# First feed-forward of a two-layer trunk: gating products and sums of gated tiles on VectorE instead of GpSimd

## The chip, the cores and the metric

The kernel runs as one program on one core of a Trainium2 chip. The metric is the device time of one execution in microseconds. It is called in one launch and does everything in it: all weights are loaded from HBM, and the result is written back.

Engines are called by the names of the profile: PE (TensorE, with its weight load PEld), DVE (VectorE), ACT (ScalarE), POOL (GpSimd) and SP (SyncE, which issues the DMAs).

## The reference

Two layers over x of 1024 tokens by 1024 channels, float32. Layer 0 has a short gated convolution, layer 1 a forgetting attention, and each ends with a SwiGLU feed-forward of hidden width 2816. All sub-layers are wrapped in a modulation by a condition vector c and a layer norm:

```python
for l in range(DEPTH):
    sh1, sc1, g1, sh2, sc2, g2 = jnp.split(c_act @ w_ada[l] + b_ada[l], N_MOD, axis=-1)
    h = modulate(x, sh1, sc1)
    ...
    x = layer_norm(DEEPNORM_ALPHA * x + g1[:, None, :] * y, ln1_g[l], ln1_b[l])
    h = modulate(x, sh2, sc2)
    y = swiglu(h, ffn_w_gate[l], ffn_w_up[l], ffn_w_down[l])
    x = layer_norm(DEEPNORM_ALPHA * x + g2[:, None, :] * y, ln2_g[l], ln2_b[l])

def swiglu(h, w_gate, w_up, w_down):
    return (jax.nn.silu(h @ w_gate) * (h @ w_up)) @ w_down
```

The change is in the first line of this swiglu, for l = 0.

## The kernel before, in words

A float32 operand is split into a high part and a rest, and a product is three matmuls (`mm3`, lines 167 to 171): high by high, high by rest, rest by high. `split_f` (line 654) makes the parts of a weight block: ACT writes the high part (line 659), DVE the rest (line 660).

The first feed-forward (`first_ffn`, line 1300) multiplies in blocks, with seven block products in place of eight. Tokens are in two halves of 512, hidden channels in 22 tiles of 128, taken as 11 pairs j. `hidden` (line 833) computes the gate and the up product of a pair in slots named M1 to M7. A slot has two products (m = 0 gate, m = 1 up), 12 matmuls of 128x512 each, into PSUM banks X, Y or Z of the pair. For the first six pairs ("early") M1 and M2 run ahead in slots of their own; then each pair has the slots M5, M6, M3, M7 and, after the M5 of the next pair, its M4. The later pairs have M1 and M2 in line as well.

After each product comes its evacuation (`evac`, line 1026). M5 and M6 only keep a partial sum (`keep_sum`, line 962, on DVE). M2, M3, M7 and M4 each finish a tile of hidden values (`out`, line 972). For m = 0, DVE adds the bank and the kept sum (line 979) and ACT applies silu (line 980). For m = 1, DVE adds again (line 999) and the result is multiplied with the silu (line 1000, on POOL). Where nothing has to be added, line 997 multiplies straight from the bank, on DVE. A finished tile is stored to HBM, and `derive` (line 1005) forms sums and differences of finished tiles (line 1008, on POOL), which are stored too, since the down projection multiplies in blocks again and wants them as operands.

Each `store` (line 866) is put off to the end of the next slot and then issued by SP (line 868). SP has one queue, in order. The same queue issues the weight loads of the hidden products (line 681), the loads of the modulation weights (`ada_lq`, line 783), the reloads of stored tiles (lines 875 and 882) and the loads of the down projection (lines 1145 and 1155).

Beside this, from slot 28 on, DVE computes the modulation vectors needed later: a quarter of a weight block per slot (`ada_quarter`, lines 260 and 262), from the loads of line 783. POOL forms the sums of weight blocks that M5, M3 and M7 need (`sums`, line 914: lines 918, 919, 921 and 923, each 128x1024), and at the start of the down projection those of line 1190.

The order in which instructions stand on each engine is fixed when the kernel is built. The build may move an instruction past others of its engine; at run time each engine takes its own in order. Tiles (`pg`) live in 47 pages of SBUF; a load into a page waits until its last reader is done.

Of the kernel before, what the change touches and what calls it, by code (L numbers as in the profile page):

```python
# [11 lines left out]
ALU = mybir.AluOpType  # L12
# [65 lines left out]
class Builder:  # L78
# [754 lines left out]
    def hidden(self, l, nearly, left):  # L833
# [3 lines left out]
        nc, T, look = self.nc, self.T, 2  # L837
        gp = nc.gpsimd
# [27 lines left out]
        def store(n, j, t):  # L866
            def fn():
                nc.sync.dma_start(self.dr[n][j * P:(j + 1) * P], t)
                self.stored.add((n, j))
            self.later(self.slot, fn)  # L870
# [93 lines left out]
        def leave(s, *names):  # L964
            for n in names:
                t = s.pop(n)
                if n in ("ya", "yb"):
                    self.later(self.slot, lambda t=t: self.drop("f", t))
                else:
                    self.drop("f", t)  # L970

        def out(j, r, half, s, m, bank, other):

            if m == 0:
                a = s["a"] = self.t("tmp", [P, HALF], tag="tA", bufs=3)
                if other is None:
                    nc.scalar.activation(a, bank, AF.Silu)
                else:
                    nc.vector.tensor_tensor(a, bank, other, op=ALU.add)  # L979
                    nc.scalar.activation(a, a, AF.Silu)  # L980
                return
            a = s.pop("a")
            if (r, half) == (0, 0):
                s["ya"] = self.fpage()
                y = s["ya"][:, 0]
            elif (r, half) == (1, 1):
                s["yb"] = self.fpage()
                y = s["yb"][:, 0]
            elif left and (r, half) == (0, 1):
                y = s["ya"][:, 1]  # L990
            elif (r, half) == (1, 0):
                self.flush(self.slot)
                y = s["yb"][:, 0]
            else:
                y = self.t("tmp", [P, HALF], tag="tB", bufs=3)
            if other is None:
                nc.vector.tensor_tensor(y, bank, a, op=ALU.mult)
            else:
                nc.vector.tensor_tensor(y, bank, other, op=ALU.add)
                gp.tensor_tensor(y, y, a, op=ALU.mult)  # L1000
            if (r, half) in asis:
                store(asis[r, half], j, y)
            derive(j, r, half, s, y)

        def derive(j, r, half, s, y):

            def tt(n, o, a, b, op=ALU.subtract):
                gp.tensor_tensor(o, a, b, op=op)
                if n:
                    store(n, j, o)  # L1010
            ya, yb = s.get("ya"), s.get("yb")
            if (r, half) == (0, 1) and not left:
                tt("M5", ya[:, 1], y, ya[:, 0])
            elif (r, half) == (1, 1):
                if left:
                    tt("M5", ya[:, 1], ya[:, 1], y, ALU.add)
                    tt("M6", yb[:, 1], ya[:, 1], ya[:, 0])
                    tt("M7", ya[:, 0], y, yb[:, 1])
                else:
                    tt("M6", yb[:, 1], y, ya[:, 1])  # L1020
                    tt("M7", ya[:, 0], yb[:, 1], ya[:, 0])
            elif (r, half) == (1, 0):
                tt("M3" if left else "M4", ya[:, 1], y, yb[:, 1])
                leave(s, "ya", "yb")

        def evac(i, m):
# [4 lines left out]
            if n == "M1":  # L1031
                keep(s, "m1", m, X)
                if e and m:
# [5 lines left out]
                    self.later(i, spill)  # L1039
            elif n == "M2" and e:  # L1040
                out(j, 0, 0, s, m, X, None)
                self.unbank(s.pop(("X", m)))
                if m:
                    leave(s, "ya")
            elif n == "M2":
                out(j, 0, 0, s, m, Z, s["m1"][:, m])
                self.unbank(s.pop(("Z", m)))
                if m:
                    leave(s, "m1")
            elif n == "M5":  # L1050
                keep_sum(s, "y5", m, Y, m1()) if e else keep(s, "y5", m, Y)
            elif n == "M6":
                keep_sum(s, "s2", m, X, m1()) if e else keep(s, "s2", m, X)
            elif n == "M3":
                if e and m:
                    s["ya"] = self.blk.pop(("b11", j)) if ("b11", j) in self.blk else None
                    if s["ya"] is None:
                        s["ya"] = self.lq_get(("b11", j))
                        self.blk.pop(("b11", j))
                out(j, 0, 1, s, m, Y, s["s2"][:, m])  # L1060
                self.unbank(s.pop(("Y", m)))
                if m:
                    leave(s, "s2")
            elif n == "M7":
                out(j, 1, 1, s, m, X, s["y5"][:, m])
                if m:
                    leave(s, "y5")
            elif n == "M4":
                out(j, 1, 0, s, m, X, m1() if e else None)
                self.unbank(s.pop(("X", m)))  # L1070
                if e and m:
                    self.lq_drop(("m1", j))
# [1056 lines left out]
```

## Time and profile before

| | us |
|---|---|
| median of 3 runs | 2519.61 (2512.10 to 2519.83) |
| the profiled execution | 2518.77 |
| its span, first to last instruction | 2517.0 |
| PE busy in the span | 2400.4 (95%) |
| DVE busy | 1497.8 (60%) |
| ACT busy | 827.3 (33%) |
| POOL busy | 860.0 (34%) |

The span is what the trace covers; the profiled execution's own time is 1.8 us longer. The first feed-forward's hidden part that the change touches runs from 510 to 911 us of the span. Shares over the whole span say little about it, since DVE is busy far more there than late in the kernel. Readings are therefore taken by stretches of the span.

### The profile page before, as it was taken

The numbers are of one execution on the slowest core, as the hardware profiler recorded it, in microseconds if no ns is written. First come the engines' busy times: TensorE is split into PE (matmuls) and PEld (weight loads), VectorE is DVE, ScalarE is ACT, GpSimd is POOL, SyncE is SP. The second block draws the span as 40 slices with busy tenths as digits, with TensorE's granted clock in tenths as the row PEclk, the third lists the DMA queues.
The fourth block names the chain that finished last, engine by engine and source line by source line (L and its number), as shares of the span: only waits on it lengthen the run. The fifth ranks groups of instructions, "written<-read, shape, count | busy, mean of one in ns | idle before, by whom it ended". The sixth has DMA issues, their size and how long they took to land. (4 is left out here: it accounts for less than half of the span.)

```text
span 2517.0 us, 29595 instructions
## 1 busy us (share of the span) xinstructions
PE 2400.4 (95%) x10905; PEld 1948.8 (77%) x10905; DVE 1497.8 (60%) x2129; ACT 827.3 (33%) x1321; POOL 860.0 (34%) x686
## 2 busy tenths in 40 slices
PE   7899999898899999999999999999999999999997
PEld 5688887687778878777777777777788888888886
DVE  5654548856788878986464667897632223232326
ACT  3311105421232333434223666665521111212113
POOL 6300002675556452343000556557330202030304
PEclk9999999999999999999999999999999999999999
DMA  8333303655575774215557555652211111111101
GB/s 269 118 101 117 92 17 97 202 163 173 174 225 173 272 249 147 83 51 194 192 179 226 174 176 145 153 133 72 67 34 51 51 51 51 51 43 50 44 32 67
DMA packets 286645, 311.95 MB, mean 124 GB/s; under 512 B 16068, under 2 KB 198548, under 8 KB 286500
## 3 DMA queue, kind: packets, MB, share of 16 engines
q1 hardware_dynamic: 274884, 284.69, 37.1%
q10 hardware_dynamic: 11616, 25.37, 2.7%
q8 instruction: 86, 1.41, 0.2%
q14 instruction: 59, 0.48, 0.1%
HBM read 252.91 MB, written 57.08 MB: 123 GB/s over the span
## 5 line engine op out<-in xcount | busy, mean ns | idle before, releaser
L169 PE MATMUL mm<-pg,pg 128*128 128x512 f32 x3004 | 1188.8, 397 | 35.8 <-DVE tA L979 11.4
L170 PE MATMUL mm<-pg,pg 128*128 128x512 f32 x3004 | 1186.1, 395 | 14.5 <-DVE pg L370 7.2
L171 PE MATMUL mm<-pg,pg 128*128 128x512 f32 x3004 | 1183.8, 394 | 3.6 <-POOL pg L368 2.6
L169 PEld LDWEIGHTS mm<-pg,pg 128*128 128x128 f32 x3004 | 571.7, 190 | 161.7 <-issue 18.2
L170 PEld LDWEIGHTS mm<-pg,pg 128*128 128x128 f32 x3004 | 571.8, 190 | 136.2 <-DVE pg L370 10.0
L171 PEld LDWEIGHTS mm<-pg,pg 128*128 128x128 f32 x3004 | 571.3, 190 | 125.2 <-POOL pg L368 4.1
L159 ACT CAST pg<-pg 128x1024 fp32r<-128x1024 f32 x144 | 150.5, 1052 | 586.2 <-PE mm L170 301.1
L660 DVE TENSOR_TENSOR pg<-pg,pg 128x1024 fp32r<-128x1024 f32 (+1 forms) x161 | 245.5, 1535 | 59.0 <-ACT pg L659 34.3
L1402 POOL TENSOR_TENSOR pg<-pg,tB 128x512 f32<-128x512 f32 x80 | 107.6, 1346 | 463.0 <-DVE tB L1400 462.1
L659 ACT CAST pg<-pg 128x1024 fp32r<-128x1024 f32 (+1 forms) x161 | 159.7, 1013 | 285.6 <-DVE pg L660 81.6
L163 DVE TENSOR_TENSOR pg<-pg,pg 128x1024 fp32r<-128x1024 f32 x124 | 154.2, 1248 | 151.9 <-ACT pg L159 149.4
L393 DVE TENSOR_TENSOR tB<-mm,tA 128x512 f32<-128x512 f32 x44 | 30.4, 692 | 215.9 <-PE mm L171 215.7
L262 DVE SCALAR_TENSOR_TENSOR ga<-pg,cact,ga 128x512 f32<-128x512 f32 x119 | 115.0, 966 | 53.9 <-DMA pg<-in_w_ada_dram 40.3
L1400 DVE TENSOR_TENSOR tB<-mm,pg 128x512 f32<-128x512 f32 x96 | 66.2, 690 | 134.7 <-PE mm L171 134.6
L1788 POOL TENSOR_SCALAR pg<-pg,st 128x512 f32<-128x512 f32 (+7 forms) x128 | 97.9, 773 | 122.1 <-DVE st L1786 116.3
L1811 DVE TENSOR_TENSOR pg<-sm,pg 128x512 fp32r<-128x512 f32 x192 | 104.1, 551 | 26.6 <-ACT pg L1810 23.8
L1810 ACT CAST pg<-sm 128x512 fp32r<-128x512 f32 x192 | 89.0, 480 | 50.8 <-PE sm L1807 48.7
L1785 ACT ACTIVATE pg<-s,st 128x512 f32<-128x512 f32 (+7 forms) x128 | 94.5, 744 | 28.3 <-DVE st L1782 19.1
L1779 DVE TENSOR_REDUCE st<-s 128x1 f32<-128x1024 f32 (+3 forms) x96 | 91.2, 951 | 15.1 <-PE s L1773 14.5
L1807 PE MATMUL sm<-ident,pg 128*128 128x128 f32 x576 | 98.6, 276 | 1.6 <-POOL pg L1788 1.3
L1190 POOL TENSOR_TENSOR pg<-pg,pg 128x1024 f32<-128x1024 f32 (+1 forms) x24 | 61.6, 2574 | 100.5 <-DVE pg L660 38.9
L1819 PE MATMUL mm<-pg,pg 128*128 128x512 f32 x192 | 80.3, 418 | 5.9 <-ACT pg L1810 4.7
(217 smaller groups left out, 2376.5 us busy)
## 6 DMA issues: line engine op xcount, KB each, us to landing
pg<-in_w_ada_dram SPq DMA_DIRECT2D x68, 512.0 KB
scr_hid<-pg SPq DMA_DIRECT2D x77, 256.0 KB
pg<-scr_hid SPq DMA_DIRECT2D x35, 512.0 KB
g<-in_w_ada_dram SPq DMA_DIRECT2D x56, 256.0 KB
pg<-in_ffn_w_gate_dram SPq DMA_DIRECT2D x56, 256.0 KB
pg<-in_ffn_w_up_dram SPq DMA_DIRECT2D x56, 256.0 KB
pg<-in_conv_w_in_dram SPq DMA_DIRECT2D x24, 512.0 KB
pg<-in_ffn_w_down_dram SPq DMA_DIRECT2D x44, 256.0 KB
```

The source lines that it names most:

```text
L159: nc.scalar.copy(hi, raw)
L163: nc.vector.tensor_tensor(lo, raw, hi, op=ALU.subtract)
L169: mm(out, lhsT=whi, rhs=xhi, start=first, stop=False, skip_group_check=skip)
L170: mm(out, lhsT=whi, rhs=xlo, start=False, stop=False, skip_group_check=skip)
L171: mm(out, lhsT=wlo, rhs=xhi, start=False, stop=last, skip_group_check=skip)
L262: eng.scalar_tensor_tensor(acc, w, s, acc, op0=ALU.mult, op1=ALU.add)
L659: nc.scalar.copy(hi[:, 0:n], flat[:, 0:n])
L660: nc.vector.tensor_tensor(lo[:, 0:n], flat[:, 0:n], hi[:, 0:n], op=ALU.subtract)
L1402: nc.gpsimd.tensor_tensor(z, z, m, op=ALU.add)
L1788: nc.gpsimd.tensor_scalar(lg[:, i], lg[:, i], s[:, i:i + 1], 1.0, op0=ALU.mult, op1=ALU.mult)
L1807: nc.tensor.transpose(p[:, j * P:(j + 1) * P], lg[j][:, kt * P:(kt + 1) * P], self.c["ident"])
L1811: nc.vector.tensor_tensor(pt[:, 1, a:], p[:, a:], pt[:, 0, a:], op=ALU.subtract)
```

## The change

Line 1000 and the helper of line 1008 move from POOL (`gp`) to DVE (`nc.vector`). The test on n goes as well; every call gives a name, so each result is stored as before. The weight sums of lines 918 to 923 stay on POOL.

```diff
             else:
                 nc.vector.tensor_tensor(y, bank, other, op=ALU.add)
-                gp.tensor_tensor(y, y, a, op=ALU.mult)
+                nc.vector.tensor_tensor(y, y, a, op=ALU.mult)
             if (r, half) in asis:
                 store(asis[r, half], j, y)
             derive(j, r, half, s, y)
@@
             def tt(n, o, a, b, op=ALU.subtract):
-                gp.tensor_tensor(o, a, b, op=op)
-                if n:
-                    store(n, j, o)
+                nc.vector.tensor_tensor(o, a, b, op=op)
+                store(n, j, o)
```

In the listings below, a row is an instruction with what it writes and reads: `pg` are pages of SBUF, `tA` and `tB` temporary tiles, `mm` banks of PSUM, `ga` and `mods` the modulation sums. Rows with a minus stand only in the kernel before, rows with a plus only in the changed one.

DVE, at the M4 slot of the fourth pair, whose line 999 starts at 623.92 us in the trace before:

```order
 L999 TENSOR_TENSOR pg_4367<-mm_717_4267,pg_4089 128x512
 L297 TENSOR_REDUCE mods_101<-sm_4454 128x4
+L1000 TENSOR_TENSOR pg_4367<-pg_4367,tA_4436 128x512
+L278 SCALAR_TENSOR_TENSOR mods_101<-mods_101,bada_192 128x4
 L260 TENSOR_SCALAR ga_4461<-pg_4375,cact_99 128x512
-L278 SCALAR_TENSOR_TENSOR mods_101<-mods_101,bada_192 128x4
+L1008 TENSOR_TENSOR pg_4286<-pg_4367 128x512
 L262 SCALAR_TENSOR_TENSOR ga_4461<-pg_4375,cact_99,ga_4461 128x512
 L962 TENSOR_TENSOR pg_4491<-mm_750_4478,pg_4332 128x512
-L262 SCALAR_TENSOR_TENSOR ga_4461<-pg_4470,cact_99,ga_4461 128x512 x2
+L262 SCALAR_TENSOR_TENSOR ga_4461<-pg_4470,cact_99,ga_4461 128x512
 L962 TENSOR_TENSOR pg_4491<-mm_752_4493,pg_4332 128x512
```

The product stands two rows behind the sum that feeds it, the difference three rows further; the evacuations of line 962 come one and two rows later than before.

POOL, around the same place (lines 918 to 923 are the weight sums):

```order
 L921 TENSOR_TENSOR pg_4329<-pg_4329,pg_4169 128x1024
-L1000 TENSOR_TENSOR tB_4323<-tB_4323,tA_4308 128x512
-L1008 TENSOR_TENSOR pg_4286<-tB_4323,pg_4286 128x512
 L923 TENSOR_TENSOR pg_4169<-pg_4129,pg_4169 128x1024
-L1000 TENSOR_TENSOR pg_4367<-pg_4367,tA_4352 128x512
-L1008 TENSOR_TENSOR pg_4367<-pg_4367,pg_4286 128x512
-L1008 TENSOR_TENSOR pg_4286<-pg_4367,pg_4286 128x512
 L918 TENSOR_TENSOR pg_4377<-pg_4377,pg_4464 128x1024
 L919 TENSOR_TENSOR pg_4467<-pg_4377,pg_4467 128x1024
-L1000 TENSOR_TENSOR pg_4367<-pg_4367,tA_4436 128x512
-L1008 TENSOR_TENSOR pg_4286<-pg_4367 128x512
 L921 TENSOR_TENSOR pg_4554<-pg_4554,pg_4467 128x1024
```

Before, the product and the difference of the M4 slot stood behind the weight sums 918 and 919; now POOL has the weight sums alone.

SP, the stores of the same two tiles (`scr_hid`) and the loads behind them:

```order
 L681 DMA pg_4467<-in_ffn_w_up_dram 128x4x128
 L783 DMA pg_4515<-in_w_ada_kv_dram 128x2x512
+L882 DMA pg_4511<-scr_hid_71 128x512
 L868 DMA scr_hid_72<-pg_4367 128x512
 L868 DMA scr_hid_74<-pg_4286 128x512
-L882 DMA pg_4511<-scr_hid_71 128x512
 L783 DMA pg_4513<-in_w_ada_kv_dram 128x2x512
```

The stores and the modulation load behind them keep their order; only one reload goes ahead of the stores.

## Rows read from the trace of the kernel before

**Rows 1.** Busy us of PE, PEld, DVE, ACT, POOL (instructions); PEclk; DMA share; GB/s.

```profile
510.00:592.00 82.00, 82.00 (x363) 67.87 (x362) 42.49 (x44) 19.92 (x23) 58.61 (x30) 1.00 0.44 140
592.00:700.00 108.00, 89.65 (x357) 72.05 (x356) 82.41 (x82) 21.36 (x25) 59.97 (x30) 0.90 0.56 181
700.00:880.00 180.00, 178.90 (x798) 147.47 (x797) 148.06 (x152) 61.11 (x81) 98.50 (x50) 0.99 0.68 226
880.00:911.00 31.00, 25.55 (x103) 19.83 (x102) 24.45 (x18) 11.55 (x12) 29.69 (x13) 0.94 0.68 253
```

**Rows 2.** Waits of PE, 592 to 700: us in total, times, longest.

```profile
PE mm L169 <- DVE tA L979: 9.4, 2, 6.0
```

**Rows 3.** Waits of DVE, 592 to 700, the same columns.

```profile
DVE ga L262 <- DMA pg<-in_w_ada_kv_dram: 11.8, 2, 7.8
...
DVE ga L262 <- DMA pg<-in_w_ada_dram: 6.1, 1, 6.1
```

**Rows 4.** DVE in order of time, 585 to 605: start, us, [idle before].

```profile
592.88 0.49 DVE L260 TENSOR_SCALAR ga<-pg,cact 128x512 f32<-128x512 f32 x1 [7.97 <-DMA pg<-in_w_ada_dram]
...
594.67 1.28 DVE L962 TENSOR_TENSOR pg<-mm,pg 128x512 f32<-128x512 f32 x2
```

**Rows 5.** Waits of SP's queue, 592 to 700: us in total, times, longest.

```profile
SPq L868 <- POOL pg L1008: 31.3, 12, 11.9
SPq L868 <- POOL pg L1000: 26.8, 6, 9.1
```

**Rows 6.** DVE in order of time, 622 to 650.

```profile
623.92 0.69 DVE L999 TENSOR_TENSOR pg<-mm,pg 128x512 f32<-128x512 f32 x1
...
626.91 3.54 DVE L262 SCALAR_TENSOR_TENSOR ga<-pg,cact,ga 128x512 f32<-128x512 f32 x2
...
641.59 0.75 DVE L262 SCALAR_TENSOR_TENSOR ga<-pg,cact,ga 128x512 f32<-128x512 f32 x1 [7.80 <-DMA pg<-in_w_ada_kv_dram]
...
646.41 1.21 DVE L660 TENSOR_TENSOR pg<-pg,pg 128x1024 fp32r<-128x1024 f32 x1
```

**Rows 7.** POOL in order of time, 625 to 645.

```profile
627.23 2.67 POOL L918 TENSOR_TENSOR pg<-pg,pg 128x1024 f32<-128x1024 f32 x1 [4.49 <-DMA pg<-in_ffn_w_up_dram]
...
632.66 2.28 POOL L1000 TENSOR_TENSOR pg<-pg,tA 128x512 f32<-128x512 f32 x1
635.03 1.29 POOL L1008 TENSOR_TENSOR pg<-pg 128x512 f32<-128x512 f32 x1
```

**Rows 8.** SP's queue in order of time, 634 to 645.

```profile
634.98 1.71 SPq L868 DMA_DIRECT2D scr_hid<-pg  x2
...
637.26 0.41 SPq L783 DMA_DIRECT2D pg<-in_w_ada_kv_dram  x1
```

**Rows 9.** Groups of DVE, 592 to 700: busy us, mean ns, idle before.

```profile
L262 DVE SCALAR_TENSOR_TENSOR ga<-pg,cact,ga 128x512 f32<-128x512 f32 x28 | 32.8, 1170 | 18.4 <-DMA pg<-in_w_ada_kv_dram 11.8 <-DMA pg<-in_w_ada_dram 6.1
L660 DVE TENSOR_TENSOR pg<-pg,pg 128x1024 fp32r<-128x1024 f32 x15 | 26.4, 1758 | 5.3 <-PE mm L170 4.2 <-ACT pg L659 1.1
```

**Rows 10.** POOL busy us in three stretches, line 1000, then line 1008.

```profile
592.00:700.00 108.00, 17.71 (x9) 0.90 0.56 181
700.00:880.00 180.00, 26.05 (x15) 0.99 0.68 226
880.00:911.00 31.00, 2.28 (x1) 0.94 0.68 253
...
592.00:700.00 108.00, 19.16 (x12) 0.90 0.56 181
700.00:880.00 180.00, 27.48 (x18) 0.99 0.68 226
880.00:911.00 31.00, 7.16 (x4) 0.94 0.68 253
```

**Rows 11.** Line 1363, two SBUF inputs: ns min/median/max, first and last start.

```profile
L1363 DVE TENSOR_TENSOR pg<-pg,pg x6: 680/682/693, 1085.2 to 1122.0; 128x512 f32<-128x512 f32 x6
```

**Rows 12.** A group of DVE, 880 to 911: busy us, mean ns, idle before.

```profile
L660 DVE TENSOR_TENSOR pg<-pg,pg 128x1024 fp32r<-128x1024 f32 x9 | 19.2, 2172 | 2.3 <-ACT pg L659 1.9 <-PE mm L170 0.5
```

## The prediction

> **What bounds the kernel now.** I read the first feed-forward by stretches first, since the change touches nothing outside it: busy time of each engine in four stretches between 510 and 911 us of the span [rows 1]. PE is busy for all of the first stretch (82.00 of 82.00 us) and for all but 1.1 us of the third. It loses time in two places: 592 to 700, where it is busy 89.65 of 108.00 us, and 880 to 911, busy 25.55 of 31.00 us. There the granted clock is lower as well, 0.90 and 0.94 against 1.00. At full clock an instruction takes 82.00 / 363 = 0.226 us, so the work of these two stretches is 357 x 0.226 = 80.6 us and 103 x 0.226 = 23.3 us. What can be won at all is therefore 108.0 - 80.6 = 27.4 us and 31.0 - 23.3 = 7.7 us.
>
> Next the waits of PE in the larger of the two: it waits for evacuations on DVE, 9.4 us of it for line 979 alone [rows 2]. So I ask what made DVE late. DVE's own waits there show two groups that end with the landing of a modulation weight load, 11.8 and 6.1 us [rows 3]. One more, of 7.97 us, ended at 592.88 [rows 4], so 0.9 us of it lie inside the stretch. In all 11.8 + 6.1 + 0.9 = 18.8 us lie inside. DVE's idle time inside is 108.0 - 82.4 = 25.6 us [rows 1], so 6.8 us are left for waits on PE and ACT.
>
> Then why the loads were late. SyncE issues the stores of gated tiles and the weight loads in one queue, and in this stretch its stores waited 31.3 us for line 1008 on POOL and 26.8 us for line 1000, 18 times, 3.2 us each on average [rows 5]. One chain can be followed from end to end. DVE had the gated sum (line 999) at 623.92 and was done with it in 0.69 us [rows 6]. POOL, which had to take the product after it, first ran two weight sums (lines 918 and 919), took line 1000 at 632.66 and line 1008 at 635.03 for 1.29 us [rows 7]. The two stores were issued between 634.98 and 636.69, and the load behind them at 637.26 [rows 8]. DVE waited 7.80 us for such a load, until 641.59 [rows 6]. A tile that was ready on DVE at 624.6 thus held a queue of loads until 636.7.
>
> The last view is the durations of DVE's instructions in this stretch. Line 262 takes 1170 ns on average and line 660 1758 ns [rows 9], while 0.75 and 1.21 us also occur [rows 6]. Two of line 262 took 3.54 us from 626.91 [rows 6], while line 918 on POOL ran for 2.67 us from 627.23 [rows 7]. DVE's instructions with two inputs in SBUF are held up while POOL works. In all that is 28 x 0.42 + 15 x 0.55 = 20.0 us of DVE time in the stretch.
>
> **What the change adds and removes.** It moves 33 products (line 1000) and 44 sums (line 1008) from POOL to DVE. The order of the changed kernel has all 77 on DVE, mostly one or two rows behind the line 999 or 997 that feeds them, and the two weight sums no longer stand ahead of them. Between 592 and 700 there are 9 + 12 = 21 [rows 10].
>
> Price of one on DVE: an instruction of this shape and kind, both inputs in SBUF, takes 682 ns by itself [rows 11]. Two evacuations of the same size in a row took 1.28 us [rows 4], so one in a queue adds about 0.60 us. That is the lower end. The upper end is 0.60 + 2.67 = 3.3 us, where a whole weight sum runs on POOL first [rows 7]. I take 0.60, since DVE's queue is dense there, and put the collisions in a term of their own. New work: 21 x 0.60 = 12.6 us.
>
> Collisions: POOL is busy 59.97 us in the stretch [rows 1], of which 17.71 + 19.16 = 36.9 us are the moved instructions [rows 10], 61%. With them goes 61% of the 20.0 us, 12.3 us. The other 7.7 us, from the weight sums, grow with DVE's work that can be held: 28 x 0.75 + 15 x 1.21 = 39.2 us now, 12.6 more after, so 7.7 x 1.32 = 10.2, or 2.5 us more. DVE's busy time becomes 82.4 + 12.6 - 12.3 + 2.5 = 85.2 us. The price on DVE is thus nearly paid by POOL's silence.
>
> Here a rule speaks against the change. By the rows, the two of line 262 were held up for 3.54 - 1.42 = 2.1 us by a sum of 2.67 us. The Trainium skill, page "SBUF — State Buffer", section "Who interferes with whom", says that a DVE instruction with two SBUF inputs contends with a GpSimd instruction that reads SBUF, and that the one issued second is blocked until the first has finished. All 77 moved instructions are of this kind. By that rule alone, with each of the nine weight sums of the stretch (lines 918 to 923) catching one new instruction for 2.67 us, the stretch would pay 24 us where I put 2.5 us. No row shows so unlucky an order.
>
> Load waits: in the chain above the store can go about 10 us earlier, and the 7.80 us wait is gone. For the others I take the mean 3.2 us that a store waited. The 6.1 leaves 2.9, the 4.0 (11.8 less 7.8) leaves 0.8, and the 7.97 leaves 4.8, all of it before 592. So 3.7 us of the 18.8 stay; the bounds are 0 and 18.8. The wait that is moved to DVE is short: line 1000 needs the activation on ACT, which was started a half product earlier, and what is queued behind it on DVE are evacuations and weight splits. What is late next is DVE itself. The stretch becomes 85.2 + 6.8 + 3.7 = 95.7 us, still above PE's 80.6. Gain: 108.0 - 95.7 = **12.3 us**, with the lost clock in it.
>
> 880 to 911: nine of line 660 take 2172 ns on average [rows 12], 9 x (2.17 - 1.21) = 8.7 us too long, beside a POOL that is busy 29.69 of 31.00 us [rows 1]. The moved instructions are 2.28 + 7.16 = 9.4 us of it [rows 10], a third, and the sums for the down projection move up by as much. A third of 8.7 is 2.9; five new instructions cost 3.0, but they stand behind the splits that PE waits for. Bounds 0 and 7.7; I take **3 us**, near the third.
>
> 700 to 880 [rows 1]: 33 new instructions, 19.8 us. Without any relief DVE goes from 148.06 to 167.9 of 180 us, and the moved instructions free POOL for 26.05 + 27.48 = 53.5 us of its 98.5. DVE's idle time covers it: 0. If that cover is gone, it is the slower rival below. 510 to 592: PE never waits, DVE is busy 42.49 of 82 us: 0. The down projection and all that follows keep their work and start earlier.
>
> Sum: 12.3 + 3 = 15.3 us. The profiled execution took 2518.77 us (span 2517.0), 0.84 below the median of the runs, 2519.61. 2518.77 - 15.3 = 2503.5, and with the 0.84, **2504.3 us**.
>
> **Rivals.** *The loads are late for another reason.* They also wait for free pages and for earlier transfers, and the store in front of them was only the last in line. Then 18.8 us stay: 85.2 + 6.8 + 18.8 = 110.8, 2.8 us worse than now, and the last stretch gives 3 back: about 2519. For it: DVE also frees those pages. Against it: in the chain above the load went out 0.6 us after the second store.
>
> *All is won.* PE is never late again: 27.4 + 7.7 = 35.1 us, about 2485. For it: the stretch 510 to 592, the same loop, by the code still without modulation work, has no idle PE at all. Against it: DVE needs 85.2 us where PE needs 80.6.
>
> *DVE becomes the bound, slower than before.* Its place is 700 to 880. DVE's idle time there is scattered between waits on ACT and PE, and if none of the 19.8 us fits into it, and new collisions eat the relief, PE idles 19.8 us more. In 592 to 700, 18.4 us of idle time came with 89.65 - 80.6 = 9.0 us of lower clock, half as much again, so 29.5 us. The gain before it shrinks to 18.8 - 3.7 - 12.6 = 2.5: 2519.6 + 27 = about 2547. It decides from where DVE is busy more than some 168 of the 180 us. The rule of the page named above, that the second instruction waits out the first, would bring it about. Against it: POOL's queue is halved.
>
> **How the numbers follow.** A measurement of this kernel tells about 0.3%, 7.6 us, from no change. Forecast 0.60; its own range is 2496 (no load wait left and 7.7 in the last stretch: 16.0 + 7.7 = 23.7) to 2512 (half the load waits, nothing in the last). Loads late anyway 0.18, all won 0.10, slower 0.12. Faster: 0.57 + 0.10 = 0.67; within 0.3%: 0.03 + 0.18 = 0.21; slower 0.12. The range reaches from all won to just above loads late anyway, 2484 to 2522, and leaves out the slower rival.
>
> **What would show it.** Right: stores that no longer wait for POOL; DVE's load waits in 592 to 700 down from 18.8 to about 4 us; line 262 below 1.0 us on average; DVE busy about 85 us for the same work; for the work of 592 to 700, 15.1 us above PE's 80.6, some 10 of them idle PE and 5 lower clock, by the ratio above. Wrong: load waits that stay while stores go early, or waits of PE on lines 979 and 962 that spread past 700.

## The result, and the profile after

The changed kernel takes 2491.07 us (median of 4 runs, 2487.81 to 2492.08); the kernel before took 2519.22 us beside it (4 runs). The ratio is 0.9892, with an interval of 0.9872 to 0.9912: faster by 28 us where 15.3 was forecast. The profiled execution took 2492.08 us, with a span of 2489.9, 27.1 less than before.

The changed kernel in the first three stretches, columns as in [rows 1]:

```profile
510.00:592.00 82.00, 82.00 (x364) 67.89 (x363) 70.14 (x71) 20.97 (x24) 28.63 (x11) 1.00 0.51 164
592.00:700.00 108.00, 104.39 (x464) 85.00 (x463) 103.66 (x116) 27.66 (x34) 30.92 (x12) 1.00 0.69 220
700.00:880.00 180.00, 175.76 (x783) 144.58 (x782) 156.15 (x182) 64.44 (x82) 56.66 (x21) 0.99 0.68 234
```

In the same 108 us from 592, PE issues 464 instructions where it issued 357, and its clock is no longer lowered. Fixed windows compare different work, though, since the changed kernel is further on. PE stands at the same place at 592 (364 instructions after 510, before 363), so the work of the old stretch is found by counting PE's instructions, 357 of them: it ends at about 676.5. The next two fences show that window, by engine, and DVE's groups in it with busy us, mean ns and idle time before them, as in [rows 9].

```profile
592.00:676.50 84.50, 80.98 (x360) 65.96 (x359) 80.99 (x93) 20.27 (x24) 22.93 (x9) 1.00 0.67 218
```

```profile
L262 DVE SCALAR_TENSOR_TENSOR ga<-pg,cact,ga 128x512 f32<-128x512 f32 x27 | 21.7, 804 | 4.3 <-DMA pg<-in_w_ada_dram 3.0 <-DMA pg<-in_w_ada_kv_dram 1.0
L660 DVE TENSOR_TENSOR pg<-pg,pg 128x1024 fp32r<-128x1024 f32 x13 | 18.0, 1385 | 0.0
L1000 DVE TENSOR_TENSOR pg<-pg,tA 128x512 f32<-128x512 f32 x5 | 10.6, 2126 | 0.2
L1008 DVE TENSOR_TENSOR pg<-pg,pg 128x512 f32<-128x512 f32 x6 | 6.3, 1052 | 0.1
L979 DVE TENSOR_TENSOR tA<-mm,pg 128x512 f32<-128x512 f32 x9 | 6.1, 683 | 0.0
```

Line 262 is down from 1170 to 804 ns and line 660 from 1758 to 1385. Five of the eight moved products take 2126 ns on average; the other three, undisturbed, take 683 ns. Idle time in front of DVE's instructions is almost gone, and what is left are two load waits. The work of 108.00 us is now done in 84.50 - 3 x 0.226 = 83.8 us: 24.2 us of the gain are here.

The waits of the changed kernel, 592 to 700, for [rows 2], [rows 3] and [rows 5] in turn (us in total, times, longest):

```profile
PE mm L169 <- DVE pg L962: 2.9, 2, 1.5
PE mm L169 <- DVE tA L979: 0.7, 2, 0.4
```

```profile
DVE ga L262 <- DMA pg<-in_w_ada_dram: 3.0, 1, 3.0
DVE ga L262 <- DMA pg<-in_w_ada_kv_dram: 1.0, 1, 1.0
DVE pg L660 <- ACT pg L659: 0.3, 1, 0.3
```

```profile
SPq L868 <- DVE pg L1008: 20.2, 11, 5.0
SPq L868 <- DVE pg L1000: 17.6, 6, 4.8
```

The stores wait for DVE now, 37.8 us in 17 waits, 2.2 us each, where they waited 58.1 us in 18 for POOL. POOL is out of these waits; the waits are not gone.

How far the gain is made by when can be read off the 68 matmuls of line 295, which both kernels issue at like places. The changed kernel has (ns min/median/max, first and last start us):

```profile
L295 PE MATMUL sm<-ident,ga x68: 270/272/328, 609.8 to 1274.3; 128*128 128x128 f32 x68
```

Before they ran from 622.7 to 1301.7, so the lead is 12.9 us at the first and 27.4 at the last. Matched one by one, the lead is 15.6 us at 649 us of the time before, 20.4 at 679, 24.7 at 706, 25.9 at 880 and 27.0 at 1190. All but some 3 us are won by 706.

### The profile page after: what moved, and what is told of

The parts are those of the page before. It is cut to its first block, busy times and chain, and to the rows that moved or that the text cites. A ratio compares the mean times of both kernels' runs of the same rounds, so it can differ in the third digit from the quotient of the medians.

```text
span 2489.9 us, 29594 instructions
## 1 busy us (share of the span) xinstructions
PE 2386.3 (96%) x10905; PEld 1939.2 (78%) x10905; DVE 1535.2 (62%) x2206; ACT 827.2 (33%) x1321; POOL 729.8 (29%) x609
## 5 line engine op out<-in xcount | busy, mean ns | idle before, releaser
L169 PE MATMUL mm<-pg,pg 128*128 128x512 f32 x3004 | 1183.4, 395 | 26.9 <-ACT pg L957 8.3
L660 DVE TENSOR_TENSOR pg<-pg,pg 128x1024 fp32r<-128x1024 f32 (+1 forms) x161 | 232.0, 1449 | 25.2 <-PE mm L170 10.8
L262 DVE SCALAR_TENSOR_TENSOR ga<-pg,cact,ga 128x512 f32<-128x512 f32 x119 | 101.3, 851 | 38.4 <-DMA pg<-in_w_ada_dram 36.0
L1810 DVE TENSOR_TENSOR pg<-sm,pg 128x512 fp32r<-128x512 f32 x192 | 104.1, 551 | 25.7 <-ACT pg L1809 23.1
L1778 DVE TENSOR_REDUCE st<-s 128x1 f32<-128x1024 f32 (+3 forms) x96 | 91.3, 951 | 15.2 <-PE s L1772 14.3
```

What stands on the lines that cost most here:

```text
L169: mm(out, lhsT=whi, rhs=xhi, start=first, stop=False, skip_group_check=skip)
L262: eng.scalar_tensor_tensor(acc, w, s, acc, op0=ALU.mult, op1=ALU.add)
L660: nc.vector.tensor_tensor(lo[:, 0:n], flat[:, 0:n], hi[:, 0:n], op=ALU.subtract)
L1810: nc.vector.tensor_tensor(pt[:, 1, a:], p[:, a:], pt[:, 0, a:], op=ALU.subtract)
```

## Experiments

Two theories were set against each other. **Q**: the loads came late, because SP's queue held them behind stores that waited for POOL; this is the chain of the prediction. **P**: POOL's work as such was the cost. Its instructions hold up those of DVE, and DVE and ACT wait for what stands in POOL's long queue. The time of each run stands beside runs of the kernel before on the same chip.

| kernel | median us | ratio to before, interval |
|---|---|---|
| changed kernel | 2491.07 | 0.9892 [0.9872, 0.9912] |
| stores issued by POOL, on before | 2531.54 | 1.0041 [1.0027, 1.0056] |
| modulation loads in ACT's queue, on before | 2514.51 | 0.9979 [0.9969, 0.9989] |
| changed, POOL kept busy | 2515.43 | 0.9982 [0.9972, 0.9991] |
| changed, stores wait for POOL | 2496.22 | 0.9900 [0.9885, 0.9914] |
| products alone on DVE | 2500.79 | 0.9921 [0.9904, 0.9937] |
| sums alone on DVE | 2513.01 | 0.9974 [0.9963, 0.9985] |
| changed, weight sums on DVE too | 2485.85 | 0.9862 [0.9847, 0.9877] |
| changed, first down sums on DVE too | 2491.47 | 0.9880 [0.9865, 0.9895] |
| changed, both | 2480.17 | 0.9836 [0.9818, 0.9855] |
| before, only the weight sums on DVE | 2503.11 | 0.9927 [0.9906, 0.9947] |
| changed kernel again | 2496.95 | 0.9897 [0.9881, 0.9913] |

The last three shared one chip, with the kernel before at 2521.24 us.

From each run's trace, how far its PE is ahead of the kernel before, in us: at 592 by the count of PE's instructions from the start (0.226 us each), then by line 295, at 706 us of the time before and at the last one.

| kernel | at 592 | at 706 | at the last |
|---|---|---|---|
| changed kernel | -0.2 | 24.7 | 27.4 |
| changed kernel again | -1.6 | 24.0 | 23.3 |
| stores issued by POOL, on before | -2.7 | 2.0 | -11.5 |
| modulation loads in ACT's queue, on before | -0.2 | 4.0 | -0.9 |
| changed, POOL kept busy | -0.2 | 14.3 | 3.4 |
| changed, stores wait for POOL | 0.9 | 21.7 | 25.3 |
| products alone on DVE | -0.5 | 13.8 | 16.0 |
| sums alone on DVE | -0.9 | 6.0 | 4.9 |
| changed, weight sums on DVE too | 6.3 | 33.4 | 28.9 |
| changed, first down sums on DVE too | -2.0 | 22.5 | 26.9 |
| changed, both | 6.3 | 36.3 | 39.3 |
| before, only the weight sums on DVE | 5.6 | 17.0 | 15.9 |

The two runs of the changed kernel differ by 4 us at the last, so a single trace says no more than that.

**Stores out of SP's queue, on the kernel before.**

```diff
-                nc.sync.dma_start(self.dr[n][j * P:(j + 1) * P], t)
+                nc.gpsimd.dma_start(self.dr[n][j * P:(j + 1) * P], t)
```

> The kernel before, with the 77 stores of gated tiles issued by POOL's own queue instead of SP's; products and sums stay on POOL. Theory Q (queue): the gain of the change comes from loads that no longer stand behind late stores in SP's queue. Then DVE's waits for modulation loads between 592 and 700 us fall from 18.8 to under 6 us, and the time is 2496 to 2506, a little above the changed kernel's 2491 since DVE is still held up by POOL. Theory P (port): the gain comes from DVE no longer being held up by POOL's 77 instructions. Then nothing is won: 2515 to 2525.

It was slower, 2531.54 us, outside both forecasts. DVE's groups from 592 to 700, then POOL's store issues:

```profile
L262 DVE SCALAR_TENSOR_TENSOR ga<-pg,cact,ga 128x512 f32<-128x512 f32 x28 | 37.4, 1336 | 5.4 <-DMA pg<-in_w_ada_dram 4.9
L660 DVE TENSOR_TENSOR pg<-pg,pg 128x1024 fp32r<-128x1024 f32 x16 | 30.1, 1883 | 10.9 <-ACT pg L659 8.5 <-PE mm L170 1.9 <-issue 0.6
```

```profile
L868 POOL DMA_DIRECT2D scr_hid<-pg x21 | 11.8, 562 | 0.9 <-POOL pg L1008 0.9
```

The load waits were cured, 18.8 to 4.9 us, and yet the lead at 706 was only 2 us. In their place came 8.5 us of waits for ACT's split, which itself waited 21.8 us for POOL's weight sums, and longer instructions. The run is not a clean one: each store takes 562 ns of POOL, which becomes busier (71.68 of 108 us), and near the end of the hidden part line 997 waits 16.1 us for a store to land. It shows that the load waits alone do not carry the gain, not what they are worth.

**Modulation loads past the stores, on the kernel before.** Here SP keeps the stores, and the loads of line 783 go out by ACT's queue.

```diff
-            self.nc.sync.dma_start(w, self.ada_cols(j, 4)...)
+            self.nc.scalar.dma_start(w, self.ada_cols(j, 4)...)
```

> The kernel before, with the modulation weight loads (line 783) issued by ACT's queue instead of SP's, so that they stand behind no store and POOL has nothing more to do. Products and sums stay on POOL. Theory Q (late loads cost the time): DVE's load waits between 592 and 700 us nearly vanish and the time is 2500 to 2510. Theory P (DVE held up by POOL, together with its full queue, costs the time): the waits vanish as well, but DVE catches up little: 2513 to 2522.

5.7 us faster than before on its chip, by the medians; the profiled execution, 2518.65 us, was the slowest of its ten. The waits from 592 to 700 show why it isn't more:

```profile
ACT pg L659 <- POOL pg L918: 14.4, 2, 10.8
DVE pg L660 <- ACT pg L659: 13.1, 4, 5.7
...
DVE ga L262 <- DMA pg<-in_w_ada_kv_dram: 5.3, 1, 5.3
DVE ga L262 <- DMA pg<-in_w_ada_dram: 5.0, 1, 5.0
```

Load waits fell by some 8 us, and DVE waited 13.1 us for ACT, which waited for POOL's line 918. DVE's idle time behind a late POOL moves from one row to another. But this run freed the modulation loads alone. The weight loads of line 681 still stood behind the stores, and the longest of these waits goes back to one of them. SP's queue, then POOL:

```profile
609.73 9.89 SPq L868 DMA_DIRECT2D scr_hid<-pg  x4
619.73 0.46 SPq L681 DMA_DIRECT2D pg<-in_ffn_w_gate_dram  x1
```

```profile
624.61 2.40 POOL L918 TENSOR_TENSOR pg<-pg,pg 128x1024 f32<-128x1024 f32 x1 [5.33 <-DMA pg<-in_ffn_w_gate_dram]
```

ACT started its split 0.03 us after this sum, having waited 10.81 us. So the run does not rule out that late stores cost time by other loads than those of line 783.

**The gain with POOL kept busy.** The changed kernel, with a POOL instruction of the old size behind each moved one; it writes a scratch tile that nobody reads.

```diff
                 nc.vector.tensor_tensor(y, y, a, op=ALU.mult)
+                gp.tensor_tensor(self.dum, y, y, op=ALU.mult)
@@
                 nc.vector.tensor_tensor(o, a, b, op=op)
+                gp.tensor_tensor(self.dum, o, o, op=op)
```

> The changed kernel, with one POOL instruction added behind each of the 77 moved ones, at the places where POOL had them before: it reads the finished tile twice and writes a scratch tile that nobody reads. POOL is as busy as before, and no store waits for it. Theory Q: 2493 to 2502; SP's stores wait for DVE only, load waits stay near 4 us. Theory P: DVE is held up as before, with 47 us more work: 2515 to 2535.

2515.43 us: of the gain of 28 us some 5 are left. The window from 592 to 700, and DVE's line 262 in it:

```profile
592.00:700.00 108.00, 97.40 (x418) 78.68 (x417) 103.77 (x110) 26.68 (x33) 57.58 (x32) 0.97 0.68 210
```

```profile
L262 DVE SCALAR_TENSOR_TENSOR ga<-pg,cact,ga 128x512 f32<-128x512 f32 x30 | 27.7, 924 | 3.4 <-DMA pg<-in_w_ada_dram 2.1 <-DMA pg<-in_w_ada_kv_dram 0.9
```

DVE is as busy as in the changed kernel and waits as little for loads (3.0 us), but gets less done: PE issues 418 instructions, not 464. The lead is 14.3 us at 706 where the changed kernel has 24.7, and 3.4 at the last of line 295. So the loads come in time, next to nobody waits for the added work, and still most is lost. Not all of it is lost in the stretch, though: with POOL as busy as before, 14.5 of some 25 us are still made from 592 to 706, and 11 are lost again later. The added work reads one tile twice and stands between the weight sums, which therefore run later too (PE waits 6.8 us for line 962), so this is not the price of hold-ups alone.

**Late stores in the changed kernel.** POOL multiplies one column of the tile by 1.0 ahead of each store but those of M1, so that stores wait for POOL's queue while POOL does little more.

```diff
+                if n != "M1":
+                    gp.tensor_scalar(t[:, 0:1], t[:, 0:1], 1.0, 1.0, op0=ALU.mult, op1=ALU.mult)
                 nc.sync.dma_start(self.dr[n][j * P:(j + 1) * P], t)
```

> The changed kernel, with one POOL instruction on a single column of the tile ahead of each store of line 868 (M1 excepted), so that the stores depend on POOL again and stand behind its weight sums, while POOL takes hardly any time of DVE. Theory Q: the stores and the loads behind them are late again, DVE waits for loads, and a third to two thirds of the gain is lost: 2500 to 2510. Theory P: 2490 to 2496.

2496.22 us, 0.2 above the range of P. That is 5 us above the changed kernel by the medians of two chips, 2 by the ratios (0.9900 against 0.9892, intervals that overlap), and 3 by the lead at 706 (21.7); at the last of line 295 the lead, 25.3, lies between those of the two runs of the changed kernel. SP's first wait and DVE's two load waits from 592 to 700 (the edit moves some lines down by two):

```profile
SPq L870 <- POOL pg L869: 44.9, 10, 13.4
```

```profile
DVE ga L262 <- DMA pg<-in_w_ada_dram: 3.3, 1, 3.3
...
DVE ga L262 <- DMA pg<-in_w_ada_kv_dram: 2.9, 2, 2.6
```

Stores wait 44.9 us for POOL, almost as long as the 58.1 before, up to 13.4 us at a time; the load waits grow to no more than 6.2. This is the cleanest test of Q: once POOL has little else to do, late stores cost 0 to 5 of 28 us. It does not test load waits as long as the 18.8 us before.

**Products alone, sums alone.** Each is one of the two lines of the change.

> The kernel before with the 33 products (line 1000) alone on DVE; the 44 sums stay on POOL, so four of six stores of a pair still wait for it. Theory Q: POOL's queue is 46 us shorter, stores are late by about half: 2503 to 2512. Theory P: 17.4 of the 38.6 us by which the 77 hold up DVE go: 45% of 28 us, 2506 to 2508.

> The kernel before with the 44 sums (line 1008) alone on DVE; the 33 products stay on POOL. Each sum on DVE then waits for a product on POOL, and what is queued behind it on DVE waits too. Theory Q: stores hardly earlier, and DVE gets a new wait: 2510 to 2530. Theory P: 21.2 of 38.6 us go, 55% of 28 us: 2503 to 2506.

Products alone: 2500.79 us, faster than either theory forecast, some 20 us won while the sums' stores waited 40.4 us for POOL in the stretch. Sums alone: 2513.01 us, in the range of Q and not in that of P, and a wait that is new:

```profile
DVE pg L1008 <- POOL pg L1000: 19.8, 7, 6.4
DVE pg L1008 <- POOL tB L1000: 14.6, 3, 10.0
```

With the product left on POOL, DVE stands still for its result, 34.4 us in the stretch. A moved step needs its producer moved with it.

**Other work moved instead.** If POOL's quantity of work is the cost, it should not matter much which lines leave it. On the kernel before, only the weight sums (lines 918 to 923) go to DVE; the gating products and sums stay on POOL.

```diff
-                gp.tensor_tensor(g(1, 0), g(1, 0), g(1, 1), op=ALU.add)
+                nc.vector.tensor_tensor(g(1, 0), g(1, 0), g(1, 1), op=ALU.add)
```

and so on for the other three.

> The kernel before, where gating products and sums stay on GpSimd and the stores go on waiting for it; only the weighted sums of the hidden tiles go to VectorE. Theory P (GpSimd's total work between 592 and 700 us is what costs, by whichever lines): 2495 to 2505 us, with VectorE's waits for modulation loads well under 18.8 us since GpSimd runs less late. Theory Q (the path product, sum, store, load is what costs): the stores still wait for GpSimd, 2510 to 2520 us, and waits for loads above 10 us.

2503.11 us, 18 us won without touching a line of the change. Of these, 5.6 us are there at 592 already (they were made before 510), and 11.4 are made from 592 to 706. The weight sums were 59.97 - 36.9 = 23.1 us of POOL's work in the stretch before; the change took away 36.9 us and won 25 there. The stretch 592 to 700, and its stores:

```profile
592.00:700.00 108.00, 95.81 (x404) 77.04 (x403) 87.13 (x99) 26.89 (x33) 38.46 (x22) 0.94 0.67 213
```

```profile
SPq L868 <- POOL pg L1008: 22.8, 12, 4.1
SPq L868 <- POOL pg L1000: 15.2, 6, 4.2
```

The stores still depend on POOL, yet they wait 38.0 us, as long as the changed kernel's stores wait for DVE (37.8). It was the length of POOL's queue that made them late. Since the stores wait less here as well, this run does not tell P from Q by itself. As to loads the expectation of P held only in part: modulation loads cost DVE 9.1 us, but DVE now waits 11.7 us for the weights of the sums as well.

**Nothing left on POOL.** The weight sums, the first chunk's sums for the down projection, and both, on top of the change.

```diff
-                tt = lambda o, a, b, op=ALU.subtract: gp.tensor_tensor(o, a, b, op=op)
+                tt = lambda o, a, b, op=ALU.subtract: (nc.vector if not left and ci == 0 and n == "M6" else gp).tensor_tensor(o, a, b, op=op)
```

> The changed kernel, with the weight sums of the hidden slots (lines 918, 919, 921, 923) on DVE too, so that POOL is silent there. Theory P: DVE pays 9 x 1.13 = 10 us between 592 and 676 us and gets back the 17 us for which the sums held it up; 2483 to 2490. If DVE's queue is the limit and not the port: 2492 to 2500.

> The changed kernel, with the first weight sums of the down projection (line 1189 of that kernel, the first chunk's M6) on DVE instead of POOL. In the changed kernel four of them run on POOL without a break from 853 to 865 us, two instructions of DVE take 2.89 and 3.35 us meanwhile, and PE waits 4.2 us for line 979. Theory P: DVE pays 4 x 1.13 = 4.5 us and gets 3.8 us back at the place that counts, and PE's wait goes: 2486 to 2490. If the evacuation is late for DVE's own work: 2491 to 2494.

> The changed kernel, with the first feed-forward's weighted sums of its hidden tiles and the first chunk's down sums also moved from GpSimd to VectorE. Theory P (what costs is VectorE held up beside GpSimd's long instructions and waiting behind GpSimd's chain): the two earlier gains add, the gap near 856 us of the run with the weighted sums alone is gone and the lead of 33 us at 706 us is kept: 2478 to 2484 us. Theory Q (what cost was the loads held behind stores in SP's queue, which the change has already cured): VectorE's added work buys nothing, 2486 to 2493 us.

> The changed kernel itself, word for word, beside the run with both further moves on the same chip: both theories expect 2489 to 2493 us.

The changed kernel missed its expectation by 4 us on this chip, where the kernel before is slower too; its ratio, 0.9897, agrees with the first. The weight sums alone bring the lead at 706 to 33.4 us, of which 6.3 are made before 510, then PE waits 8.5 us at 855.77. The first down sums alone take away the gap near 860 that the changed kernel has, but that run is 2 us behind at 592, as the second run of the changed kernel is, and the time stays (2491.47, a ratio of 0.9880 whose interval overlaps that of the changed kernel). Both together take 2480.17 us (2478.91 to 2484.03), 16.8 us below the changed kernel on the same chip, 2496.95 (2493.34 to 2497.40): the fastest version here. Some 7 of these 16.8 us are made before 510, by the count of PE's instructions. From 592 to 700 PE has no idle time at all:

```profile
592.00:700.00 108.00, 108.00 (x488) 89.37 (x487) 100.78 (x142) 31.80 (x40) 0.00 (x0) 1.00 0.73 228
```

142 instructions of DVE take less time here than 116 in the changed kernel. One pair of rows shows it at its plainest. DVE in order of time (start, us) with the weight sums moved, where POOL runs four sums of the down projection in one piece, 11.43 us from 842.60:

```profile
842.87 2.88 DVE L1000 TENSOR_TENSOR tB<-tB,tA 128x512 f32<-128x512 f32 x1
845.68 3.40 DVE L660 TENSOR_TENSOR pg<-pg,pg 128x1024 fp32r<-128x1024 f32 x1
...
855.03 0.68 DVE L979 TENSOR_TENSOR tA<-mm,pg 128x512 f32<-128x512 f32 x1
```

And the same instructions with both moved, where POOL is silent:

```profile
840.00 0.69 DVE L1000 TENSOR_TENSOR tB<-tB,tA 128x512 f32<-128x512 f32 x1
840.60 1.22 DVE L660 TENSOR_TENSOR pg<-pg,pg 128x1024 fp32r<-128x1024 f32 x1
...
843.47 0.68 DVE L979 TENSOR_TENSOR tA<-mm,pg 128x512 f32<-128x512 f32 x1
```

Between them, in both runs, stand a sum (line 1008) and another split. From the product to the start of line 979 it is 12.2 us beside POOL and 3.5 us without. PE waits for that line 979.

## Why the prediction was right, and where its sizes were not

Sign and place held: faster, nearly all of it between 592 and 700, DVE not the bound. The size was partly luck: 2491 lies below the forecast's own range of 2496 to 2512, and inside the stated range only because that reaches down to the rival that all is won.

The mechanism held in part. The forecast's 12.3 us are 15.1 of load waits that go, put down to stores that no longer wait for POOL, less 2.8 more of DVE's own work. The load waits did go. But POOL's long queue of work is the cause that the runs bear out; the stores are one of its ways, and were given too much weight. The signs that came (stores that no longer wait for POOL, load waits of 4.0 us, line 262 at 804 ns) did not tell the two apart. Three terms of the sum were mis-sized.

**592 to 700: 24.2 us, not 12.3.** The prediction's 95.7 us were 85.2 busy, 6.8 of waits on PE and ACT, and 3.7 of load waits. The window of 84.50 us has 80.99 busy and 3.5 idle. Term by term:

- *Waits on PE and ACT, 6.8.* They were carried over unchanged, and that step failed: almost nothing is left: no wait on PE or ACT is listed in the window, and beside the load waits 0.7 us are idle. Most were waits for PE (lines 660 and 979), which itself waited for DVE; that they went because DVE was no longer late is argued, not tested. This is 6 of the 12 us missing.
- *DVE busy, 85.2.* The total came near for the wrong reasons. 82 + 21 = 103 instructions were to be done there, and 93 are. The ten that are not, two each of lines 660, 962 and 999 and of the moved ones and one each of 260 and 262, are worth 2 x (1.39 + 0.69 + 0.68 + 0.68) + 0.48 + 0.80 = 8.2 us at undisturbed or mean durations, and most had been done before 592. The hold-ups were dearer, by the following.
- *Collisions.* Line 262 (27 x 0.05 = 1.4 us), line 660 (13 x 0.18 = 2.3) and the moved ones (5 x 1.44 + 6 x 0.37 = 9.4) are 13.1 us too long, where 7.7 + 2.5 = 10.2 were put. Lines 262 and 660 are almost free now; the new ones, put at 2.5, pay 9.4. So POOL's silence gave DVE back 20.0 - 13.1 = 6.9 us for 12.6 us of new work, about half the price and not nearly all of it. Line 278, which the sum left out, was held up as well: three of it took 1621 ns each, before 1256, 1.1 us more in all.
- *510 to 592, put at 0.* PE loses nothing there before or after, so the stretch was passed over. But DVE does 27 instructions more in it, 70.14 us busy against 42.49, 21 of them moved ones. Before, it waited 18.6 us there for ACT's splits (line 659); after, that wait is gone. A stretch without idle PE can still be where another engine gets ahead. The 8.2 us moved out, less 2.9 for the dearer collisions and 1.1 for line 278, bring DVE's busy time 4.2 us below the 85.2.
- *Load waits, 3.7 of 18.8 left.* 4.0 are listed, 2.8 of them inside the window, since the first began at 590.8: right in size. The step behind it was right only in part. At the place that was followed, the tile of line 999 was ready at 624.6 before and the load behind its stores went out at 637.26, 12.7 us later. In the changed kernel, DVE:

```profile
613.96 0.68 DVE L999 TENSOR_TENSOR pg<-mm,pg 128x512 f32<-128x512 f32 x1
...
615.16 2.87 DVE L1000 TENSOR_TENSOR pg<-pg,tA 128x512 f32<-128x512 f32 x1
617.95 2.35 DVE L278 SCALAR_TENSOR_TENSOR mods<-mods,bada 128x4 f32<-128x4 f32 x1
...
620.62 0.68 DVE L1008 TENSOR_TENSOR pg<-pg 128x512 f32<-128x512 f32 x1
```

and SP's queue and POOL there:

```profile
618.06 3.59 SPq L868 DMA_DIRECT2D scr_hid<-pg  x2
621.99 0.38 SPq L783 DMA_DIRECT2D pg<-in_w_ada_kv_dram  x1
```

```profile
615.10 2.39 POOL L918 TENSOR_TENSOR pg<-pg,pg 128x1024 f32<-128x1024 f32 x1 [7.05 <-DMA pg<-in_ffn_w_up_dram]
617.56 2.73 POOL L919 TENSOR_TENSOR pg<-pg,pg 128x1024 f32<-128x1024 f32 x1
```

The load goes out 7.4 us after the tile was ready, so 5.3 us were won, not some 10: the product stands beside line 918, and line 278, ahead of the difference, beside line 919. What the stores are worth depends on POOL. With POOL silent, late stores cost 0 to 5 us in all, and the load waits stay at 6.2. With POOL kept busy, stores that go out early keep the load waits at 3.0 and 14.5 of the 25 us of the stretch, but hardly anything in the end. So either cure takes most of the load waits away, the 15.1 us can't be credited to the stores alone, and only the runs with a shorter queue on POOL keep the gain.

These rows also bear on the rule that was weighed. The product began 0.06 us behind line 918 and ended 0.54 us after it; line 278, on a tile of 128x4, lasted 2.35 us beside line 919. The Trainium skill, page "SBUF — State Buffer", section "Who interferes with whom", says that the second of two such instructions is blocked until the first is done, and these rows agree. By that rule with every weight sum catching a new instruction 24 us were to be paid; the new instructions paid 9.4, nearly four times the 2.5 and less than half of the 24. What reads PSUM goes free here: line 979 takes 683 ns, as before.

**880 to 911: about 1 us, not 3.** The lead grows from 25.9 at 880 to 27.0 at 1190; in the second run of the changed kernel it falls there, from 25.2 to 24.4. The same work now lies at 854 to 885 us, where DVE's group of line 660 is:

```profile
L660 DVE TENSOR_TENSOR pg<-pg,pg 128x1024 fp32r<-128x1024 f32 x8 | 14.9, 1875 | 0.5 <-PE mm L170 0.5
```

It took 2172 ns before [rows 12], so only a third of the 0.96 us by which it was too long is gone. POOL's sums for the down projection (line 1190 before, 1189 now) moved up, as was said, and the first four now run in one piece:

```profile
853.23 11.67 POOL L1189 TENSOR_TENSOR pg<-pg,pg 128x1024 f32<-128x1024 f32 x4 [27.22 <-DMA pg<-in_ffn_w_down_dram]
```

```profile
853.72 2.89 DVE L1008 TENSOR_TENSOR pg<-tB,pg 128x512 f32<-128x512 f32 x1
856.54 3.35 DVE L660 TENSOR_TENSOR pg<-pg,pg 128x1024 fp32r<-128x1024 f32 x1
859.82 0.68 DVE L979 TENSOR_TENSOR tA<-mm,pg 128x512 f32<-128x512 f32 x1
```

```profile
860.55 0.80 PE L169 MATMUL mm<-pg,pg 128*128 128x512 f32 x1 [4.22 <-DVE tA L979]
```

A moved sum and a split were held up, line 979 stood behind them, and PE waited 4.22 us. The prediction had the move and not its collision.

**The rivals.** Loads late for another reason: no, 4.0 us are left. All won (2485): nearer than the forecast; in 592 to 700, 24.2 of its 27.4 us came. DVE as the bound in 700 to 880: DVE is busy 156.15 us of 180, PE's waits from 700 to 911 are the 4.2 above and 2.8 at 885.55, and the time it needed, 2547, is far off.

**What stays open.** The shares of POOL's two effects, hold-ups of DVE and waits behind its queue (those of the stores among them), can't be told apart: the run that kept POOL busy also delayed the weight sums, the cures overlap, and no run on the kernel before frees the stores and all loads without giving POOL or ACT other work. Why the run with POOL kept busy loses 11 us of its lead after 706 is not shown either.

## What to carry to other kernels

When two engines share a stage, the cost of work on the slower one is not its own busy time but what it does to the other: look for instructions of one shape with two durations, and for a wait that moves to another row when one wait is cured. Waits that sit behind the same late engine are one budget, and are sized together; a stretch without idle time on the bottleneck may still be where others gain the lead. Work that moves should move with its producer, and its new place be looked up beside what the other engine still runs.

## What the runs showed of the hardware that was not expected

A DVE instruction on a tile of 128x4 (line 278) takes 0.15 us with POOL silent (at 845.87 in the version with both moved) and 2.33 us beside a POOL sum (at 862.60 in the changed kernel): the hold-up has the length of POOL's instruction, not of its own. The 128x1024 weight sums that take POOL 2.4 to 2.9 us take DVE 1.22 us, so a kernel with them on DVE needs less of DVE's time in all (100.78 us for 142 instructions, against 103.66 for 116). A store issued by POOL costs POOL 562 ns.
